# Two unused slivers of SBUF that move tiles by 64 and 160 bytes

## The chip, the cores and the metric

The kernel runs on one core of a Trainium2 chip. The metric is the device time of one execution in microseconds (us). SBUF is the on-chip memory of 128 partitions; a tile has the same byte offset in every partition, so one number says where it lies. The engines are named as in the profile: PE (TensorE), PEld (its loads of the stationary operand), DVE (VectorE), ACT (ScalarE), POOL (GpSimd) and SP (SyncE, whose queue issues most DMAs).

## The reference

One layer of an encoder on 256 tokens with 4096 channels: a layer norm, one input projection (4096 x 13312) that feeds a gated short convolution and a windowed attention, one output projection (4096 x 4096), a residual, and a second layer norm.

```python
h = layer_norm(x, emb_ln_g, emb_ln_b)
p = h @ w_in                       # c_b, c_c, c_h, c_z, q, k, v, a_z
y_conv = c_b * centred_short_conv(c_c * c_h, conv_w) * silu(c_z)
y_attn = banded_window_attention(q, k, v, sink) * silu(a_z)
y = concatenate([y_conv, y_attn], -1) @ w_out
out = layer_norm(alpha * h + y, ln_g, ln_b)
```

Everything is float32.

## The kernel before

The two projections are nearly all of the work. Float32 operands are split in two parts, hi (`fp32r`) and lo (what hi leaves over), and a product is made of three matmuls: x_hi times w_hi, x_hi times w_lo, x_lo times w_hi. I call these three a triple. The tokens are the stationary operand: `xT` holds, for each of 32 blocks of 128 channels, the 256 tokens' hi and lo parts (2048 bytes a block), first of the normalised x and later of the mixer's output y. The weights are the moving operand and stream in from HBM in tiles of 8192 bytes a partition.

The work is a list of steps written out by hand (`IN_STEPS`, `OUT_STEPS`), one weights' tile each:

- A plain step ("s") loads a 1 MiB tile `w`, splits it into `whi` (ACT, L200) and `wlo` (DVE, L204), and runs four blocks of channels against 512 output columns for both halves of the tokens: 8 triples, 24 matmuls of 512 columns (`mm`, L242 to L244, in the input projection; `mm_out`, L908 to L910, in the output projection). The last two output chunks are 256 columns wide.
- A pair step ("S") takes two blocks of channels with a scheme of seven products in place of eight (`mm_pair`, L266 to L268). Half a tile is loaded, DVE makes three sums of weights' blocks (`sums`, L181 to L183), and the split works on 1792 elements. Seven triples of 256 columns follow, in the order xT, xT, sum, xT, sum, xT, sum in the input projection: where it says sum, the stationary operand is a sum of x blocks out of `SC` (with a second tile `SC2`). In the output projection these are sums of y blocks in `SCy`, which take one xT place more.

A step's split is made three steps ahead of its matmuls. Between steps stand the attention of each head group (`scores` L551 to L553, `pv` L606 to L608), transposes (L481, L592), the convolution and the gates. The program's order is by hand (`manual_schedule`), engine by engine.

Tiles get their places from pools. The pools stand one behind the other in SBUF, and a pool has one place for each tile's name, in the order of first use:

```python
    const = ctx.enter_context(tc.tile_pool(name="const", bufs=1))
    wpool = ctx.enter_context(tc.tile_pool(name="wpool", bufs=3))
    small = ctx.enter_context(tc.tile_pool(name="small", bufs=4))
```

`const` (with `xT`) comes first, then `wpool` (three buffers each of `whi` and `wlo`, and `w0` to `w2`), then `small` (tiles of 4 to 8 bytes), and behind it all pools opened later: `psc` with SC, SC2 and SCy, `pa` with the attention's tiles, `pc`, `pw`, and R, which takes the residual and some weights' tiles of the output projection. Within their tiles, the slices that a matmul reads begin at multiples of 512 bytes, so all slices of a tile have the tile's remainder by 128:

| tile | starts at byte | remainder by 128 |
|---|---|---|
| xT | 17280 | 0 |
| whi, wlo, w (9 places of 8192) | 82880 and on | 64 |
| SC, SCy | 157408 | 96 |
| SC2 | 173792 | 96 |
| kT, v, pT, qhl (attention), R, hT, x | 157408 and on | 96 |

Of the kernel before, what the change touches and what calls it, by code (L numbers as in the profile page):

```python
# [8 lines left out]
F32 = mybir.dt.float32  # L9
# [5 lines left out]
P = 128  # L15
# [83 lines left out]
def encoder_kernel(ctx: ExitStack, tc: tile.TileContext, x, emb_g, emb_b, wi, ws, conv_w, sink, wo, ln_g, ln_b, out):  # L99
# [3 lines left out]
# [3 lines that stand above are left out]
# [115 lines left out]
    musd = const.tile([P, 2, 4], F32, name="musd")  # L221
    eps_t = const.tile([P, 1], F32, name="eps_t")
    nc.vector.memset(eps_t, LN_EPS)


    acc = {}
# [894 lines left out]
```

## Time and profile before

| | |
|---|---|
| runs | 1533.02, 1534.77, 1535.11 us; median 1534.77 us |
| profiled execution | span 1532.5 us from the first to the last instruction; no time beside it is given |
| PE busy | 1518.5 us, 99% |
| DVE, ACT busy | 1329.9 us (87%), 780.7 us (51%) |
| DMA | 315.65 MB, mean 206 GB/s |

The span is 2.3 us under the median of the runs. A line of a group has the source line, the engine, the operation, the tile written and those read, the shape, the count, then the busy time in us, the mean of one in ns, and the engine's idle time before them with what ended it. In a line of the timeline the first number is the start in us from the span's start and the second the duration. Matmuls overlap: one starts while the one before it still drains, so the distance between starts is the pace, and the duration is longer than that.

### The profile page before, as it was taken

To read this page: it belongs to the slowest core of one execution; us is meant where nothing else is said; L and a number is where in the kernel's file an instruction comes from. 1 tells how busy PE (TensorE), PEld (TensorE's weight loads), DVE (VectorE), ACT (ScalarE), POOL (GpSimd) and SP (SyncE) were. 2 spreads that over 40 slices of the span, in tenths; PEclk is the share of its full clock that TensorE was granted. 3 is DMA by queue.
4 is the path that set the end of the run, shared out by engine and by line. 5 is a ranking of instruction groups with operands and counts; after the bars stand their busy time and mean duration, and the time that the engine had idled before them with its cause. 6 is when DMAs were issued, how large, how long until landed. Compare 5 with 4: busy or idle time off the path is not lost.

```text
span 1532.5 us, 21818 instructions
## 1 busy us (share of the span) xinstructions
PE 1518.5 (99%) x8879; PEld 1330.7 (87%) x8879; DVE 1329.9 (87%) x1555; ACT 780.7 (51%) x669; POOL 1.3 (0%) x7
## 2 busy tenths in 40 slices
PE   7999999999999999999999999999999999999998
PEld 4888889989998988889888889888988888888897
DVE  7769889899899898898898999989898688888876
ACT  4545546656566555545455445544456344443431
POOL 0000000000000000000000000000000000000000
PEclk9999999999999999999999999999999999999999
DMA  7545554555555555656555555556557756666663
GB/s 290 205 179 192 207 197 163 204 179 203 203 177 181 183 178 205 231 185 234 188 190 208 209 195 196 204 183 228 206 193 287 268 188 226 250 206 225 213 239 140
DMA packets 71716, 315.65 MB, mean 206 GB/s; under 512 B 8544, under 2 KB 12608, under 8 KB 50880
## 3 DMA queue, kind: packets, MB, share of 16 engines
q1 hardware_dynamic: 70608, 312.43, 57.2%
q10 hardware_dynamic: 1008, 1.84, 0.3%
q8 instruction: 69, 1.13, 0.3%
q14 instruction: 31, 0.25, 0.0%
HBM read 305.23 MB, written 8.91 MB: 205 GB/s over the span
## 4 chain that ended last, share of the span: by engine, by line
PE 96%; DVE 2%; DMA 1%; ACT 0%; SPq 0%; issue 0%; ACTq 0%
PE acc L242 15%; PE acc L243 15%; PE acc L244 15%; PE acc L908 6%; PE acc L910 6%; PE acc L909 6%; PE pacc L267 6%; PE pacc L266 6%; PE pacc L268 5%; PE acc L267 4%; PE acc L266 4%; PE acc L268 4%; PE att L481 1%; DVE wlo L204 1%; DMA w<-in_ws 0%; DVE st L319 0%
## 5 line engine op out<-in xcount | busy, mean ns | idle before, releaser
L200 ACT ACTIVATE whi<-w 128x2048 fp32r<-128x2048 f32 (+1 forms) x354 | 621.3, 1755 | 628.1 <-DVE w L183 213.5
L204 DVE TENSOR_TENSOR wlo<-w,whi 128x2048 fp32r<-128x2048 f32 (+1 forms) x354 | 736.5, 2083 | 129.3 <-ACT whi L200 128.8
L242 PE MATMUL acc<-whi,xT 128*128 128x512 f32 x988 | 391.1, 396 | 0.0
L243 PE MATMUL acc<-wlo,xT 128*128 128x512 f32 x988 | 387.6, 392 | 0.0
L244 PE MATMUL acc<-whi,xT 128*128 128x512 f32 x988 | 386.2, 391 | 0.0
L244 PEld LDWEIGHTS acc<-whi,xT 128*128 128x128 f32 x988 | 185.6, 188 | 41.5
L243 PEld LDWEIGHTS acc<-wlo,xT 128*128 128x128 f32 x988 | 185.6, 188 | 38.2 <-DVE wlo L204 1.7
L242 PEld LDWEIGHTS acc<-whi,xT 128*128 128x128 f32 x988 | 185.7, 188 | 36.1
L908 PE MATMUL acc<-whi,xT 128*128 128x512 f32 (+1 forms) x480 | 176.0, 367 | 0.0
L910 PE MATMUL acc<-whi,xT 128*128 128x512 f32 (+1 forms) x480 | 175.2, 365 | 0.0
L909 PE MATMUL acc<-wlo,xT 128*128 128x512 f32 (+1 forms) x480 | 174.6, 364 | 0.2 <-DVE wlo L204 0.2
L181 DVE TENSOR_TENSOR w<-w 128x512 f32<-128x512 f32 x179 | 122.3, 683 | 8.7 <-DMA w<-in_ws 8.7
L910 PEld LDWEIGHTS acc<-whi,xT 128*128 128x128 f32 x480 | 90.1, 188 | 15.7
L909 PEld LDWEIGHTS acc<-wlo,xT 128*128 128x128 f32 x480 | 90.1, 188 | 15.5 <-DVE wlo L204 0.9
L267 PE MATMUL acc<-wlo,xT 128*128 128x256 f32 x370 | 103.3, 279 | 0.0
L266 PE MATMUL acc<-whi,xT 128*128 128x256 f32 x370 | 103.1, 279 | 0.0
L268 PE MATMUL acc<-whi,xT 128*128 128x256 f32 x370 | 103.1, 279 | 0.0
L908 PEld LDWEIGHTS acc<-whi,xT 128*128 128x128 f32 x480 | 90.2, 188 | 14.0 <-issue 0.4
L266 PE MATMUL pacc<-whi,xT 128*128 128x256 f32 x350 | 99.4, 284 | 0.0
L267 PE MATMUL pacc<-wlo,xT 128*128 128x256 f32 x350 | 97.8, 279 | 0.0
L268 PE MATMUL pacc<-whi,xT 128*128 128x256 f32 x350 | 97.6, 279 | 0.0
L267 PE MATMUL pacc<-wlo,SC 128*128 128x256 f32 x330 | 93.0, 282 | 0.0
(230 smaller groups left out, 2055.2 us busy)
## 6 DMA issues: line engine op xcount, KB each, us to landing
w<-in_wi SPq DMA_DIRECT2D x112, 1024.0 KB
w<-in_ws SPq DMA_DIRECT2D x202, 512.0 KB
w<-in_wo SPq DMA_DIRECT2D x41, 1024.0 KB
R<-in_wo SPq DMA_DIRECT2D x13, 1024.0 KB
x<-in_x SPq DMA_DIRECT2D x7, 512.0 KB
yl<-yd SPq DMA_DIRECT2D x7, 512.0 KB
xc<-in_x SPq DMA_DIRECT2D x14, 256.0 KB
R<-in_ws SPq DMA_DIRECT2D x6, 512.0 KB
```

The source lines that it names most:

```text
L181: nc.vector.tensor_tensor(s01, b22, b12.to_broadcast([P, 2, HW]), op=ALU.add)
L200: nc.scalar.activation(part(j, wh[j]), part(j, raw[j]), AF.Copy)
L204: nc.vector.tensor_tensor(part(j, wl[j]), part(j, raw[j]), part(j, wh[j]).bitcast(F32), op=ALU.subtract)
L242: nc.tensor.matmul(a, xh, hk, start=(first and k == 0), stop=False)
L243: nc.tensor.matmul(a, xh, lk, start=False, stop=False)
L244: nc.tensor.matmul(a, xl, hk, start=False, stop=(last and k == PK - 1))
L266: nc.tensor.matmul(o, ah, hi[:, w, :], start=(opens and p == 0), stop=False)
L267: nc.tensor.matmul(o, ah, lo[:, w, :], start=False, stop=False)
L268: nc.tensor.matmul(o, al, hi[:, w, :], start=False, stop=(closes and last))
L908: nc.tensor.matmul(o, yh, hk, start=first, stop=False)
L909: nc.tensor.matmul(o, yh, lk, start=False, stop=False)
L910: nc.tensor.matmul(o, yl, hk, start=False, stop=last)
```

## The change

Two tiles are allocated that nothing writes or reads: 64 bytes a partition at the end of `const`, and 96 bytes in `small`.

```diff
     musd = const.tile([P, 2, 4], F32, name="musd")
     eps_t = const.tile([P, 1], F32, name="eps_t")
     nc.vector.memset(eps_t, LN_EPS)
+    const.tile([P, 16], F32, name="gap")
+    small.tile([P, 24], F32, name="gap2", bufs=1)
```

The instructions of the built program are the same on every engine, in the same order and with the same waits; only line numbers behind the two new lines are higher by two. What moves is where tiles start:

| tile | start before | start after | remainder by 128 before, after |
|---|---|---|---|
| xT | 17280 | 17280 | 0, 0 |
| whi, wlo, w | 82880 | 82944 | 64, 0 |
| SC, SCy | 157408 | 157568 | 96, 0 |
| SC2 | 173792 | 173952 | 96, 0 |
| kT, v, pT, qhl, R, hT, x | 157408 and on | 160 more | 96, 0 |

By 256, xT has the remainder 128, the weights' tiles go from 192 to 0, and SC goes from 224 to 128. The end of the used space moves from byte 229088 to 229248 of a partition.

## The prediction

> **What bounds the kernel now.** I read first the page's busy times and its chain, then the groups with one shape to a row, then the timeline of TensorE around changes of pace.
>
> ```profile
> span 1532.5 us, 21818 instructions
> PE 1518.5 (99%) x8879; PEld 1330.7 (87%) x8879; DVE 1329.9 (87%) x1555; ACT 780.7 (51%) x669; POOL 1.3 (0%) x7
> PEclk9999999999999999999999999999999999999999
> PE 96%; DVE 2%; DMA 1%; ACT 0%; SPq 0%; issue 0%; ACTq 0%
> ```
>
> TensorE (PE) is busy for 99% of the span, at a granted clock that never falls under 0.9, and 96% of the chain that ended last is its own work. Nothing else can shorten the kernel by much: only how closely one matmul follows another counts. The groups say how many there are.
>
> ```profile
> L242 PE MATMUL acc<-whi,xT 128*128 128x512 f32 x988 | 391.1, 396 | 0.0
> L908 PE MATMUL acc<-whi,xT 128*128 128x512 f32 x368 | 144.8, 393 | 0.0
> L181 DVE TENSOR_TENSOR w<-w 128x512 f32<-128x512 f32 x179 | 122.3, 683 | 8.7 <-DMA w<-in_ws 8.7
> ```
>
> L242 and L908 are the first matmul of a triple (hi times hi, hi times lo, lo times hi), so there are 988 + 368 = 1356 triples with 512 columns, or 4068 matmuls. Pair steps are counted by their sums on DVE at L181: 179 steps of seven triples with 256 columns (the few that read R are left out of every sum here). The mean in a row (396 ns at L242) holds the drain and overlaps the next matmul, so the pace has to be read from starts.
>
> ```profile
> 1187.24 0.40 PE L909 MATMUL acc<-wlo,xT 128*128 128x512 f32 x1
> ...
> 1263.92 0.28 PE L266 MATMUL pacc<-whi,xT 128*128 128x256 f32 x1
> ...
> 1473.78 0.28 PE L908 MATMUL acc<-whi,xT 128*128 128x256 f32 x1
> ...
> 1503.70 0.28 PE L908 MATMUL acc<-w,xT 128*128 128x256 f32 x1
> ...
> 1504.49 0.28 PE L908 MATMUL acc<-w,xT 128*128 128x256 f32 x1
> ...
> 1511.56 0.28 PE L908 MATMUL acc<-whi,xT 128*128 128x256 f32 x1
> ```
>
> From the first row up to the second 335 matmuls start: 76.68 us / 335 = 228.9 ns for 512 columns. Between the next two there are 264: 29.92 / 264 = 113.3 ns for 256 columns. Between the last two there are 60: 7.07 / 60 = 117.8 ns, for the same code, the same shapes and tiles with the same address remainders. So TensorE has at least two paces for 256 columns, 340 and 353.3 ns a triple. It went from the quick one to the slow one at a wait (the six matmuls from 1503.70 to 1504.49 take 0.79 us where 0.68 would do) and stayed there. A third stretch shows that 512 columns have two paces as well.
>
> ```profile
> 192.89 0.40 PE L242 MATMUL acc<-whi,xT 128*128 128x512 f32 x1
> ...
> 204.09 0.28 PE L266 MATMUL pacc<-whi,xT 128*128 128x256 f32 x1
> ```
>
> Here 48 matmuls take 11.20 us, 233.3 ns each: 700 ns a triple where the long stretch has 686.7. The distance is 13.3 ns a triple both times. What decides the pace inside a pair step shows in one of them; I quote the first matmul of each of its triples.
>
> ```profile
> 764.64 0.28 PE L266 MATMUL pacc<-whi,xT 128*128 128x256 f32 x1
> ...
> 764.98 0.28 PE L266 MATMUL acc<-whi,xT 128*128 128x256 f32 x1
> ...
> 765.33 0.28 PE L266 MATMUL acc<-whi,SC 128*128 128x256 f32 x1
> ...
> 765.69 0.28 PE L266 MATMUL acc<-whi,xT 128*128 128x256 f32 x1
> ...
> 767.10 0.27 PE L481 MATMUL att<-ident,ug 128*128 128x128 f32 x1
> ```
>
> Two triples with xT as the stationary tile take 0.34 and 0.35 us; the first with SC takes 0.36, and the four after it (765.69 to 767.10) take 1.41, 0.353 each. The step comes in at the quick pace and loses it at the first SC triple.
>
> In the 88 triples from 1473.78, all on xT, the quick pace lasted until a wait. This is the one sign in the profile that a place in SBUF matters: SC's slices begin 96 bytes past a multiple of 128, xT's at one.
>
> **The change part by part.** It adds no instruction and takes none away, and every engine keeps its order and its waits, so no queue, DMA or semaphore has a cost of its own: 0, with nothing to hide. What moves is addresses.
>
> ACT and DVE: the split of a weights' tile reads w, 64 past a multiple of 128, or R, 96 past it.
>
> ```profile
> L200 ACT ACTIVATE whi<-w 128x2048 fp32r<-128x2048 f32 x152 | 291.8, 1920 | 236.1 <-PE acc L244 77.4 <-PE acc L910 74.7 <-issue 43.6
> L200 ACT ACTIVATE whi<-R 128x2048 fp32r<-128x2048 f32 x13 | 24.9, 1919 | 18.5 <-PE acc L910 13.0 <-PE pacc L268 4.8 <-DMA R<-in_wo 0.8
> L204 DVE TENSOR_TENSOR wlo<-w,whi 128x2048 fp32r<-128x2048 f32 x152 | 347.7, 2287 | 82.4 <-ACT whi L200 82.2
> L204 DVE TENSOR_TENSOR wlo<-R,whi 128x2048 fp32r<-128x2048 f32 x13 | 29.7, 2284 | 1.1 <-ACT whi L200 1.1
> ```
>
> 1920 against 1919 ns and 2287 against 2284: two remainders, one price. I take 0 for both engines.
>
> DMA: the waits for a landing are few.
>
> ```profile
> DVE w L181 <- DMA w<-in_ws: 8.7, 4, 3.2
> ```
>
> If rows on the grid land sooner, at most the 8.7 us of DVE's waiting goes, and TensorE, busy for all but 1532.5 - 1518.5 = 14 us, sees little of it. I take 0, and 8.7 us either way as the ends.
>
> TensorE's pace is the whole sum. From below: nothing changes, 0. From above: every pair step keeps the quick pace throughout, 179 x 7 x 13.3 ns = 16.7 us. A loss is bounded by the 512-column triples all at 700 ns: 1356 x 13.3 ns = 18.1 us. With SC on xT's grid, what knocks the pace down in the step at 764.64 is gone; but a step must also come in quick, and tiles on one grid can run at the slow pace, as here.
>
> ```profile
> 279.60 0.28 PE L551 MATMUL att<-kT,qhl 128*128 128x256 f32 x1
> ...
> 280.31 0.28 PE L266 MATMUL pacc<-whi,xT 128*128 128x256 f32 x1
> ```
>
> These six score matmuls take 0.71 us, 118 ns each, though both their tiles lie 96 past a multiple of 128 and so on one grid with each other: a common grid alone doesn't bring the quick pace back. I therefore take half of the upper bound, 8.4 us, for steps that come in quick and stay so, or that never leave a quick stretch. It is a choice between ends, not a measured share. The sum is 1532.5 - 8.4 = 1524.1 us of span. The median of the runs, 1534.77, stands 2.3 us over the span of the profiled execution; so 1526.4, and I say 1526 us.
>
> What is late next: DVE is busy for 1329.9 us, 86.8%, and would be at 87.3% of a span of 1524, so it still covers. The longest pace gain would shorten a pair step from 7 x 353.3 ns = 2.47 us to 7 x 340 ns = 2.38 us, while DVE's work for such a step (split 2.02, sums 0.68 and twice 0.43, since L183 has the shape of L182) is 3.56 and leans on the longer 512-column steps beside it, 24 x 228.9 ns = 5.49 us.
>
> ```profile
> L204 DVE TENSOR_TENSOR wlo<-w,whi 128x1792 fp32r<-128x1792 f32 x179 | 361.0, 2020 | 43.1 <-ACT whi L200 42.9
> L182 DVE TENSOR_TENSOR w<-w 128x256 f32<-128x256 f32 x179 | 76.1, 425 | 6.2
> ```
>
> **The rivals.** First, no change. The paces are states into which waits throw TensorE, and addresses play no part; the SC triple is slow for another reason, such as the jump to another tile. For it: the two stretches from 1473.78 and from 1504.49 have different paces on equal remainders. Against it: the quoted step drops exactly at SC. It gives 1534.8, give or take a microsecond or two. The Trainium skill, SBUF — State Buffer, section "Who interferes with whom", speaks for this rival and against any gain: TensorE has two read ports of its own, one for the moving operand and one for loading weights, and waits on nobody. By that rule the sum would be 1534.8; no run so far contradicts it outright.
>
> Second, a slower kernel. The 700 ns state of the 512-column triples becomes more common, because the weights' slices now come in at another phase against xT's. For it: that state exists (192.89 to 204.09). Its price is 13.3 ns a triple, so it decides from 0.2% of the time, 3.1 us, or 230 of 1356 triples more in it; at two thirds of them it costs 12 us and gives 1547. Against it: 1187 to 1264 has none of it.
>
> Third, a large gain. The 512-column pace itself has an address part, because each slice of the weights begins 64 bytes off a multiple of 128 and touches one block of 128 bytes more than it fills. One such block in 17 of the 228.9 ns is 13.5 ns; 4068 x 13.5 ns = 54.9 us, so 1480. Against it: the slices of 256 columns are off by as much, one block in nine, and yet run at 113.3 ns, just under half of 228.9. The Trainium skill, TensorE: Matmul & The Clock Gate, section "Wait — 56ns, not 53.3ns?", has 215.7 ns from start to start for 512 columns; the trace has 228.9, so 13.2 ns is unaccounted for by that page, which would be 53.7 us here and is an estimate from the page's figure.
>
> **How the numbers follow.** A gain of 0.2% to 1.2% by pair steps at the quick pace: 0.40, the likeliest, so 1526 us, with 1516 to 1531 as its own range. No change: 0.37. Slower: 0.16. The large gain: 0.07. About 0.2% (3.1 us) is what a measurement of this kernel can tell from no change. Faster is then 0.40 + 0.07 = 0.47, same 0.37, slower 0.16. The range runs from 1510, which leaves out the large gain, to 1539, which leaves out the slower cases over 4 us, some 0.10; together under 0.2.
>
> **What would show it.** In the changed kernel's timeline SC triples should no longer start the slow pace: steps that come in at 0.34 should end their seven triples in 2.38 us, not 2.47. The rows at L200 and L204 should keep 1920 and 2287 ns. If the pace of 512 columns leaves 228.9 in either direction, the second or third rival holds and my number is wrong. If SC still knocks a quick step down, my mechanism is wrong whatever the time does.

## The result and the profile after

The changed kernel takes 1549.64 us (median of 4 runs, 1549.47 to 1549.8) where the kernel before takes 1534.67 (1533.02 to 1535.11): a ratio of 1.0098, 95% interval 1.0084 to 1.0113. It is slower by 15 us. The page's first lines and its chain:

```profile
span 1547.8 us, 21818 instructions
PE 1534.1 (99%) x8879; PEld 1336.7 (86%) x8879; DVE 1330.2 (86%) x1555; ACT 780.6 (50%) x669; POOL 1.3 (0%) x7
PEclk9999999999999999999999999999999999999999
PE 98%; DMA 1%; DVE 1%; ACT 0%; SPq 0%; issue 0%; ACTq 0%
```

TensorE is busy 15.6 us longer with the same 8879 instructions at the same granted clock, and the span is 15.3 us longer. ACT and DVE do the same work in the same time. The groups with one shape to a row confirm it for the splits, whose operands moved too:

```profile
L200 ACT ACTIVATE whi<-w 128x2048 fp32r<-128x2048 f32 x152 | 291.7, 1919 | 252.8 <-PE acc L246 82.5 <-PE acc L912 69.1 <-issue 50.2
L204 DVE TENSOR_TENSOR wlo<-w,whi 128x2048 fp32r<-128x2048 f32 x152 | 347.7, 2287 | 91.3 <-ACT whi L200 91.3
```

1919 and 2287 ns, against 1920 and 2287 before. So the loss is in how closely matmuls follow each other. TensorE's timeline at the ends of the two stretches that the prediction counted in:

```profile
1197.71 0.39 PE L911 MATMUL acc<-wlo,xT 128*128 128x512 f32 x1
...
1275.55 0.29 PE L268 MATMUL pacc<-whi,xT 128*128 128x256 f32 x1
...
1487.59 0.28 PE L910 MATMUL acc<-whi,xT 128*128 128x256 f32 x1
...
1527.45 0.27 PE L952 MATMUL att<-ident,t 128*96 128x128 f32 x1
```

From the first row to the second 335 matmuls of 512 columns start: 77.84 us / 335 = 232.4 ns, where the same 335 took 228.9 before. From the third to the fourth 336 matmuls of 256 columns start: 39.86 / 336 = 118.6 ns, and the first 264 of them have 118.6 too; before, those 264 had 113.3. A pair step, by the first matmul of each of its seven triples:

```profile
771.18 0.28 PE L268 MATMUL pacc<-whi,xT 128*128 128x256 f32 x1
...
771.54 0.28 PE L268 MATMUL acc<-whi,xT 128*128 128x256 f32 x1
...
771.90 0.28 PE L268 MATMUL acc<-whi,SC 128*128 128x256 f32 x1
...
772.26 0.28 PE L268 MATMUL acc<-whi,xT 128*128 128x256 f32 x1
...
772.61 0.28 PE L268 MATMUL pacc<-whi,SC 128*128 128x256 f32 x1
...
772.97 0.28 PE L268 MATMUL pacc<-whi,xT 128*128 128x256 f32 x1
...
773.32 0.28 PE L268 MATMUL pacc<-whi,SC 128*128 128x256 f32 x1
...
773.68 0.60 PE L483 MATMUL att<-ident,ug 128*128 128x128 f32 x4
```

0.36 for the first triple, on xT, and 2.50 us for all seven. The quick pace of 0.34 isn't lost at SC here; it is never there: no triple of 256 columns in this kernel takes less than 0.347 us.

For all that follows I add up, over the whole timeline, the distances from the start of a triple to the start of what comes next, and take the mean of those without a wait (those under 1.5 ns a column). By that sum, 512-column triples go from 687.7 to 698.0 ns, which over 1356 of them is 14.0 us, and 256-column triples from 352.4 to 356.1, which over 1423 (the plain ones at the end among them) is 5.2 us. Waits inside triples shrink from 7.4 to 4.5 us. Together that is 16.3 us more; all that lies outside the triples takes some 1 us less, and the span grew by 15.3.

### The profile page after: what moved, and what is told of

Its sections match the earlier page's. It is cut to its first block, busy times and chain, and to the rows that moved or that the text cites. A ratio compares the mean times of both kernels' runs of the same rounds, so it can differ in the third digit from the quotient of the medians.

```text
span 1547.8 us, 21818 instructions
## 1 busy us (share of the span) xinstructions
PE 1534.1 (99%) x8879; PEld 1336.7 (86%) x8879; DVE 1330.2 (86%) x1555; ACT 780.6 (50%) x669; POOL 1.3 (0%) x7
## 4 chain that ended last, share of the span: by engine, by line
PE 98%; DMA 1%; DVE 1%; ACT 0%; SPq 0%; issue 0%; ACTq 0%
PE acc L244 15%; PE acc L245 15%; PE acc L246 15%; PE acc L910 7%; PE acc L911 7%; PE acc L912 7%; PE pacc L268 6%; PE pacc L270 6%; PE pacc L269 6%; PE acc L270 4%; PE acc L269 4%; PE acc L268 4%; PE att L483 1%; DMA x<-in_x 1%; PE att L594 0%; PE acc L371 0%
## 5 line engine op out<-in xcount | busy, mean ns | idle before, releaser
L912 PEld LDWEIGHTS acc<-whi,xT 128*128 128x128 f32 x480 | 90.3, 188 | 16.3
L270 PE MATMUL pacc<-whi,SC 128*128 128x256 f32 x330 | 93.0, 282 | 0.0
```

What stands on the lines that cost most here:

```text
L270: nc.tensor.matmul(o, al, hi[:, w, :], start=False, stop=(closes and last))
L912: nc.tensor.matmul(o, yl, hk, start=False, stop=last)
```

## The experiments

Every kernel below is the kernel before with tiles allocated in another order or with unused slivers between them; only the thirteenth changes an access. A ratio compares with the kernel before as it was measured again beside that run; these medians lie between 1534.55 and 1535.63 us. The first question is which of the two moves costs the time, and whether a place or a distance matters.

**The 64-byte sliver alone** (weights move as in the changed kernel, SC goes to another place off the grid):

```diff
+    const.tile([P, 16], F32, name="gap")
```

> The 64-byte sliver alone: weights' tiles go from 64 to 0 past a multiple of 128, SC from 96 to 32. If the weights' place sets TensorE's pace, nearly the whole loss is here: 1547 to 1551 us, and 512-column triples near 698 ns as in the changed kernel. If SC's place does it, 1533 to 1537 us with 512-column triples at 687 ns. If paces are only states that any disturbance reshuffles, no rule holds and the time may lie anywhere from 1530 to 1550.

Measured: 1549.76 us, ratio 1.0099 (1.0084 to 1.0114), 512-column triples at 698.4 ns. The whole loss comes with the weights' tiles.

**SC alone onto xT's grid, weights as before:**

```diff
+    small.tile([P, 8], F32, name="gap2", bufs=1)
```

> A sliver of 32 bytes behind the weights alone: SC goes from 96 to 0 past a multiple of 128, weights stay at 64 as before. If the weights' place sets the pace, 1533 to 1536 us. If SC's place costs the 15 us, 1547 to 1551 us. If SC on xT's grid keeps pair steps at the quick pace, as the prediction had it, 1518 to 1530 us.

Measured: 1528.20 us, ratio 0.9956 (0.9940 to 0.9973). This is the gain that the prediction expected of SC. Its page, and two pair steps, one behind the other:

```profile
span 1526.5 us, 21818 instructions
PE 1508.1 (99%) x8879; PEld 1316.4 (86%) x8879; DVE 1329.6 (87%) x1555; ACT 781.3 (51%) x669; POOL 1.3 (0%) x7
```

```profile
773.59 0.28 PE L267 MATMUL pacc<-whi,xT 128*128 128x256 f32 x1
...
774.29 0.28 PE L267 MATMUL acc<-whi,SC 128*128 128x256 f32 x1
...
774.65 0.28 PE L267 MATMUL acc<-whi,xT 128*128 128x256 f32 x1
...
775.00 0.28 PE L267 MATMUL pacc<-whi,SC 128*128 128x256 f32 x1
...
775.34 0.28 PE L267 MATMUL pacc<-whi,xT 128*128 128x256 f32 x1
...
776.02 0.28 PE L267 MATMUL pacc<-whi,xT 128*128 128x256 f32 x1
...
776.70 0.28 PE L267 MATMUL acc<-whi,SC 128*128 128x256 f32 x1
...
777.04 0.28 PE L267 MATMUL acc<-whi,xT 128*128 128x256 f32 x1
...
778.40 0.39 PE L243 MATMUL acc<-whi,xT 128*128 128x512 f32 x1
```

The second step comes in quick and stays so: its SC triple at 776.70 takes 0.34 us and the step 2.38, so SC no longer knocks the pace down. The first step comes in slow, with 0.70 us for two triples on xT and 0.36 for the first SC triple at 774.29, and is quick from the second SC triple at 775.00 on, 0.34. That is the rule in this kernel: of its 185 pair steps 114 come in quick (a first triple of 340 ns, where the others have 350 or more), and in all 185 the fifth triple, an SC triple, is quick. Before, only seven steps came in quick, the one at 764.64 among them, and no SC triple took less than 349 ns. So in its new place SC also brings the quick pace back.

Over the kernel, SC triples fall from 354.6 to 341.9 ns and 256-column triples on xT from 350.9 to 343.0, and 256-column triples take 13.8 us less in sum. The 512-column ones take 4.9 us more, at an unchanged pace (687.2), because plain steps now wait for DVE's half of the split, and the attention's product with v (`pv`) takes 2.8 us more. Together that is the 6.0 us by which the span is shorter, to a tenth. The lists of waits have, for the loads of the stationary operand before the second matmul of a triple in the input projection, first before and then in this kernel:

```profile
PEld acc L243 <- DVE wlo L204: 1.7, 7, 0.3
```

```profile
PEld acc L244 <- DVE wlo L204: 7.8, 25, 0.7
```

1.7 us in 7 waits has become 7.8 in 25. So part of the gain is handed to the next bound.

**Place or distance.** Two kernels put a sliver of 64 bytes ahead of xT. In the first, xT and the weights change places by 128 (xT 64, weights 0), and their distance stays that of the kernel before; in the second, all lie at 64, with the changed kernel's distance.

```diff
+    const.tile([P, 16], F32, name="gap0")
     xT = const.tile([P, KT, 2 * S], F32R, name="xT")
...
+    small.tile([P, 8], F32, name="gap2", bufs=1)
```

> A sliver of 64 bytes ahead of xT: xT at 64, weights at 0, SC at 64 past a multiple of 128. Weights and xT lie as far from each other as in the kernel before, by 128, but each on the other's place. If the distance between the two operands sets the pace, 1533 to 1536 us (687 ns a 512-column triple). If the moving operand's own place does, as in the changed kernel, 1547 to 1551 us (698 ns).

Measured: 1528.22 us, ratio 0.9958 (0.9943 to 0.9973). The expectation of 1533 to 1536 left out that SC was on xT's grid here, so that the kernel to compare with is the one at 1528.20. The 512-column triples are at 687.5 ns.

```diff
+    const.tile([P, 16], F32, name="gap0")
     xT = const.tile([P, KT, 2 * S], F32R, name="xT")
...
+    const.tile([P, 16], F32, name="gap")
+    small.tile([P, 24], F32, name="gap2", bufs=1)
```

> Slivers ahead of xT and behind it: xT, weights and SC all at 64 past a multiple of 128, so on one grid as in the changed kernel, but off the multiples of 128. If the distance between operands sets the pace, 1547 to 1551 us (698 ns). If the moving operand's own place does, as in the kernel before, 1533 to 1536 us (687 ns).

Measured: 1550.79 us, ratio 1.0106 (1.0090 to 1.0121), 698.1 ns. The distance from the stationary to the moving operand sets the pace of the 512-column triples, and the places themselves make no difference that shows: 687.5 against 687.2 ns at one distance, 698.1 against 698.0 at the other. Nor does the place where the weights' rows land: at 0 past a multiple of 256 the kernel takes 1528.22 us, at 192 it takes 1528.20.

**Other distances.** xT and SC at 0 by 128, with the weights at 32, at 96, and at 64 but 128 bytes further up:

```diff
# weights at 32 past a multiple of 128
+    const.tile([P, 24], F32, name="gap")
+    small.tile([P, 16], F32, name="gap2", bufs=1)
# weights at 96
+    const.tile([P, 8], F32, name="gap")
# weights at 64, 128 bytes further up
+    const.tile([P, 32], F32, name="gap")
+    small.tile([P, 8], F32, name="gap2", bufs=1)
```

> xT and SC at 0, weights at 32 past a multiple of 128. If only distance 0 is bad and every other one good, 1526 to 1530 us. If the pace depends on the distance step by step, something between 1528 (distance 64) and 1550 us (distance 0), some 1539. If only a whole 64 is good, 1547 to 1551 us.

> xT and SC at 0, weights at 96 past a multiple of 128. Same theories as for 32: 1526 to 1530 us if only distance 0 is bad, some 1539 us if step by step, 1547 to 1551 us if only a whole 64 is good. A time unlike that of weights at 32 would say that the sign of the distance counts.

> As the run with SC alone moved to 0 and weights at 64 (1528 us), but the weights' tiles lie 128 bytes further up, so their distance to xT by 256 is another one. If the pattern repeats every 128 bytes, 1526 to 1530 us. If it repeats every 256 bytes or not at all, another time: up to 1550 us.

Measured: 1553.07, 1552.75 and 1541.81 us (ratios 1.0120, 1.0118 and 1.0046, the last with 1.0031 to 1.0061). The first two are slower than any case that was expected; the nearest is the one in which only a whole 64 is good. The last is no repeat of 1528: its 512-column triples are at 699.7 ns, while its 256-column ones stay near the quick pace, 346.6 on xT. A remainder by 128 doesn't describe the 512-column pace; 192 by 256 is another distance than 64.

**SC at another distance, weights as before:**

```diff
+    small.tile([P, 24], F32, name="gap2", bufs=1)
```

> Weights at 64 and SC at 64 past a multiple of 128, xT at 0: SC lies at distance 0 from the weights, xT at 64. If distance 0 slows a triple whatever its stationary tile, the SC triples come to 355 ns or more while the 512-column triples stay at 687: 1534 to 1540 us. If SC's distance from xT or weights counts only as a change of the distance from triple to triple, about as before, 1533 to 1536 us.

Measured: 1535.37 us, ratio 1.0006 (0.9996 to 1.0016). SC triples are at 358.6 ns, 512-column triples at 688.1. A triple's pace goes with the distance to its own stationary tile, and a slow SC triple takes the xT triples beside it along: they are at 351.1 where a good SC leaves them at 343.0.

**Distances 0 and 32, and 64 by other multiples of 256.** The order of the tiles in `const` is changed (told here in short, not as a diff):

```text
# distance 0: musd and eps_t ahead of xT
     order: ident, cw, sk, musd, eps_t, xT; small "gap2" of 96 bytes
# distance 32
     order: ident, cw, sk, eps_t, xT, musd; small "gap2" of 64 bytes
# distance 320
     order: ident, xT, musd, eps_t, cw, sk; small "gap2" of 32 bytes
# distance 576
     order: cw, sk, xT, ident, musd, eps_t; small "gap2" of 32 bytes
```

> musd and eps_t are allocated ahead of xT, so that the weights' tiles begin exactly at distance 0 from xT by 512 (before: 64; the changed kernel: 128), SC keeps the good place of 1528 us. If a true common grid is the good or bad thing about the changed kernel, distance 0 goes like 128: 1547 to 1551 us. If the pace has its own value at each distance by 512, any time from 1525 to 1555; a 512-column triple near 647 ns (three times 215.7) would give some 1475 us.

> Distance 32 by 512. If only a distance in odd multiples of 64 is good, 1547 to 1555 us, like 96 and 160. If small distances are good and those over 64 bad, 1520 to 1530 us.

> cw and sk are allocated behind xT: distance 320, which is 64 by 256. If the pattern repeats every 256 bytes, 1526 to 1530 us with 512-column triples at 687 ns. If it repeats only every 512 bytes or not, another time, 1530 to 1555 us.

> ident, musd and eps_t lie behind xT: distance 576, which is 64 by 512, with xT, weights and SC in other places than in any kernel so far. If the distance by 512 sets the pace, 1526 to 1530 us, with 512-column triples at 687 and pair steps' triples at 340 to 343 ns. If the whole distance matters, another time.

Measured: 1532.05, 1546.85, 1527.46 and 1527.57 us. 320 and 576 give what 64 gives (687.4 ns, and 343.0 on xT at 256 columns, both of them): as far as these two show it, the distance counts by 256. So 128, the changed kernel's distance, is not the same as 0. At 0 the two shapes part, and the timeline shows it:

```profile
1185.42 0.40 PE L910 MATMUL acc<-wlo,xT 128*128 128x512 f32 x1
...
1261.39 0.28 PE L267 MATMUL pacc<-whi,xT 128*128 128x256 f32 x1
...
1469.65 0.28 PE L909 MATMUL acc<-whi,xT 128*128 128x256 f32 x1
...
1509.97 0.27 PE L951 MATMUL att<-ident,t 128*96 128x128 f32 x1
```

75.97 us / 335 = 226.8 ns for 512 columns, quicker than before (228.9); 40.32 / 336 = 120.0 ns for 256 columns, slower than the slow pace of 117.8 before.

**Both distances in one kernel.** The kernel at distance 0, with the split weights of pair steps written 192 bytes lower in `whi` and `wlo` (a pair step fills 1792 of their 2048 elements), which makes 64 by 256 of them. The few pair steps on the third part of R keep their place.

```diff
     def part(j, t):
 
+        if is_pair(j) and len(raw[j].shape) == 2 and t is not raw[j]:
+            moved.add(j)
+            return t[:, HW - 48:PIECE - 48]
...
-        hi, lo = (t.pop(j).rearrange("p (b w) -> p b w", w=HW) for t in (wh, wl))
+        hi, lo = (t.pop(j) for t in (wh, wl))
+        k0 = 1 if j in moved else 0
+        hi, lo = ((t[:, HW - 48:PIECE - 48] if k0 else t).rearrange("p (b w) -> p b w", w=HW) for t in (hi, lo))
...
-            nc.tensor.matmul(o, ah, hi[:, w, :], start=(opens and p == 0), stop=False)
+            nc.tensor.matmul(o, ah, hi[:, w - k0, :], start=(opens and p == 0), stop=False)
```

The other two matmuls of a triple take `w - k0` in the same way.

> The kernel with distance 0 (1532 us), but pair steps put their split weights 192 bytes lower in the same tiles, so that plain steps run at distance 0 and pair steps at 64 by 256, within one kernel. If the distance of each matmul's own two operands sets its pace, 512-column triples keep 682 ns and pair steps' triples fall from 357 to 343 ns: 1521 to 1526 us, the lower end if no more of the gain is lost to waits than with SC alone moved. If the place of the tiles sets it, both keep their paces of distance 0: 1531 to 1533 us. If a change of distance between steps throws the paces off, slower than both, over 1533 us.

Measured: 1525.62 us, ratio 0.9936 (0.9920 to 0.9953), the fastest of all. Its timeline has both paces:

```profile
773.11 0.28 PE L274 MATMUL pacc<-whi,xT 128*128 128x256 f32 x1
...
775.49 0.39 PE L248 MATMUL acc<-whi,xT 128*128 128x512 f32 x1
...
1179.16 0.40 PE L917 MATMUL acc<-wlo,xT 128*128 128x512 f32 x1
...
1255.13 0.28 PE L274 MATMUL pacc<-whi,xT 128*128 128x256 f32 x1
```

A pair step in 2.38 us, and 335 matmuls of 512 columns in 75.97. Over the kernel 512-column triples have 682.1 ns and pair triples on xT at distance 64 have 345.4. The distance of each matmul's own operands counts, not the place of a tile as a whole. It also parts two readings of SC: xT and SC lie as they do in the kernel at distance 0, and with the weights' slices alone moved SC triples go from 357.6 to 341.3 ns. So SC has to fit the weights, not xT. The time is near the slow end of what was expected: waits for the split have grown here too (8.8 us for wlo in the input projection).

**Distance 224:**

```text
     order: ident, sk, musd, xT, eps_t, cw; small "gap2" of 128 bytes
```

> Distance 224 by 256, the one multiple of 32 not yet tried. If odd multiples of 32 are all bad, as 32, 96 and 160 were, 1545 to 1554 us. If the pace improves smoothly towards 0 from below, 1530 to 1540 us.

Measured: 1551.63 us, ratio 1.0105 (1.0090 to 1.0121); it goes with the odd multiples of 32.

All of them together. The distance is the start of the weights' slice less that of the stationary slice, by 256; the triples are means without waits, in ns; the 256-column mean on xT holds pair and plain steps, but pair steps alone in the row of both distances.

| kernel | to xT | 512 columns | 256, xT | to SC | 256, SC | us |
|---|---|---|---|---|---|---|
| before | 64 | 687.7 | 350.9 | 224 | 354.6 | 1534.67 |
| changed | 128 | 698.0 | 356.7 | 128 | 355.3 | 1549.64 |
| 64-byte sliver alone | 128 | 698.4 | 356.0 | 224 | 355.4 | 1549.76 |
| SC alone | 64 | 687.2 | 343.0 | 192 | 341.9 | 1528.20 |
| xT 64, weights 0 | 64 | 687.5 | 342.3 | 192 | 341.8 | 1528.22 |
| all at 64 | 128 | 698.1 | 357.0 | 128 | 355.6 | 1550.79 |
| weights at 32 | 160 | 702.7 | 354.5 | 160 | 353.4 | 1553.07 |
| weights at 96 | 96 | 699.8 | 357.2 | 224 | 355.6 | 1552.75 |
| weights 128 up | 192 | 699.7 | 346.6 | 192 | 344.2 | 1541.81 |
| SC at 64 | 64 | 688.1 | 351.1 | 128 | 358.6 | 1535.37 |
| distance 0 | 0 | 681.9 | 356.4 | 128 | 357.6 | 1532.05 |
| distance 32 | 32 | 699.6 | 349.7 | 160 | 354.8 | 1546.85 |
| distance 320 | 64 | 687.4 | 343.0 | 192 | 342.0 | 1527.46 |
| distance 576 | 64 | 687.4 | 343.0 | 192 | 342.0 | 1527.57 |
| both distances | 0, pairs 64 | 682.1 | 345.4 | 192 | 341.3 | 1525.62 |
| distance 224 | 224 | 699.8 | 355.0 | 96 | 355.7 | 1551.63 |

At 256 columns a mean can mix paces, so two readings stand beside it. Triples of 340 ns occur at distances 64 and 192 alone; at every other one the shortest takes 344 ns or more. And in the plain steps at the end, where no SC triple comes between, the means are 340.6 to 343.7 ns at 64, 350.1 at 32, 352.2 at 192 and 354.9 to 360.0 at the others, so the slow pace there is not SC's doing alone. At 192 these plain triples run at 340 or 353 ns, as they do at 64, but mostly at the slower.

## Why the prediction was wrong

- **The bound was right.** TensorE's pace is the whole sum: 15.6 us more of its busy time, 15.3 us more of span.
- **The step that failed** is in the part on TensorE's pace: "With SC on xT's grid, what knocks the pace down in the step at 764.64 is gone". The sum gave SC's move the whole effect, 8.4 us of gain, and put the 512-column triples at nothing, because the stretch from 1187 to 1264 had none of the 700 ns state; but that stretch shows the old distance alone. Their term measured 14.0 us of loss, and that of the 256-column triples 5.2 us of loss instead of a gain. The weights are the moving operand of every triple, so their move from 64 to 128 by 256 changed the distance in all of them: 10.3 ns on each of 1356 triples, and the quick pace at 256 columns is gone everywhere. Reading remainders by 128 led there, since by 128 the changed kernel puts everything "on one grid"; the runs have a period of 256, in which 128 and 0 are different distances.
- **SC was read rightly in part, and the size was luck.** With the weights left alone, SC's new place brought 6.4 us (1528.20 against the 1534.55 measured beside it), where the working had 8.4 of at most 16.7. But it halved the bound because "a step must also come in quick", and that condition isn't one: 71 of 185 steps come in slow in that kernel, and all are quick by the fifth triple. So 13.8 us came off the 256-column triples, near the bound, and more than half of it was lost again in the 512-column steps and the attention. The step at 764.64 was also a rare one, one of seven of 185. Nor is a common grid with xT what SC needs: with both 192 from the weights (the kernel with weights 128 up) or both 128 (the changed kernel), SC and xT share one grid, and SC triples take 344.2 and 355.3 ns. And nothing of the gain can show in the changed kernel: with the weights 128 from xT, SC at 128 or 224 is the same (1549.64, 1549.76).
- **The warning in the working was not taken.** The score matmuls, with both operands on one grid at the slow pace, were quoted and only halved the gain. Their distance is 0 by 256, and at 0 the 256-column pace is slow in the runs too (120.0 ns). Both their tiles move together in all sixteen kernels, and their pace stays: medians of 118 to 120 ns.
- **The second rival came nearest**, with 1547 and its bound of 18.1 us; the 512-column triples cost 14.0. Its form was a little off: not the 700 ns state more often, but a mixture of 690 to 706 that averages 698.0. It had a chance of 0.16, and the range was cut at 1539, below the rival's own price of 1547.
- **The first rival**, no change, falls: the same instructions take 681.9 to 702.7 ns a triple by nothing but addresses. It leant on the Trainium skill, SBUF — State Buffer, section "Who interferes with whom", by which "PE and ACT never wait on anyone". The runs don't contradict that sentence, since the work of ACT and DVE doesn't set the pace here (below); but that nothing else in SBUF could then slow TensorE doesn't follow from it, and on that the measurement decides.
- **The third rival falls too.** Neither weights that start on a multiple of 128 nor any distance gave more than about 2 ns a matmul of 512 columns; the best pace is 226.8 ns. No run reached the 215.7 of the Trainium skill, TensorE: Matmul & The Clock Gate, section "Wait — 56ns, not 53.3ns?".
- **ACT, DVE and DMA** were costed at nothing, and nothing of theirs shows in the changed kernel. That DVE "still covers" held only in part where a gain came: with SC alone moved, the loads' waits for wlo in the input projection went from 1.7 to 7.8 us. And 117.8 ns a matmul are 353.5 ns a triple, not 353.3; no term moves by more than 0.3 us for that.

What the pace is made of inside TensorE stays open. In the changed kernel, 512-column triples during which both ACT and DVE work have 698.0 ns (702 of them), with DVE alone 698.1 (574), with ACT alone 697.6 (41), and with neither 698.9 (only 8); so the work of these two isn't it. The loads of the stationary operand last the same in all sixteen kernels by the profile, 187.6 to 188.3 ns in the mean. That the stream of the moving operand and the load of the next stationary operand get in each other's way would fit a dependence on their distance, but no run shows it.

## What to carry to other kernels

Where TensorE is the bound, read its pace from start to start, and for each shape apart: here the mean duration of a triple's first matmul in the input projection went from 396 to 397 ns while a triple's pace went from 687.7 to 698.0. Work out the distance between the two operands' start addresses by 256 before adding a small tile ahead of them, and choose it for each shape by a run; a sliver that looks tidy by 128 can move every matmul to a worse distance. A sign read off one tile (SC) says nothing on moving its partner, so move one operand at a time.

## What the runs showed of the hardware

For triples of `fp32r` matmuls with a new stationary load for each, the start-to-start pace depends on the distance between the two operands' start addresses. For 512 columns a triple takes 681.9 ns at distance 0, 687 to 688 at 64, and 698 to 703 at 32, 96, 128, 160, 192 and 224. The distance counts by 256 as far as that was tried: 320 and 576 go like 64 (687.4 both). For 256 columns only 64 and 192 reach 340 ns; the means at the other distances are 350 to 360.

The pace also has a memory. Before, each of the 14 SC triples (distance 224) that came right behind a quick triple was slow, and so was every triple behind it in its step. In the kernel with SC alone moved (distance 192), 68 of the 121 SC triples that came right behind a slow triple were quick, and 453 of the 454 behind a quick one. That is why moving SC alone sped up the xT triples beside it, from 350.9 to 343.0 ns.
